# Down-weight sums spread over a forgetting attention, two stores behind the first biases, one transposition moved

## The chip, the cores and the metric

The kernel runs on one core of a Trainium2 chip. A core has TensorE (PE) for matrix products and transpositions, VectorE (DVE), ScalarE (ACT), GpSimd (POOL) and SyncE (SP). Each engine works through its own list of instructions in order; semaphores hold an instruction until what it reads has been written, and until the buffer that it writes is free. SyncE issues transfers here, and GpSimd issues some too; both kinds run on the same 16 DMA engines. The metric is the device time of one execution in microseconds (us), as the median over runs.

## The reference

The kernel computes a trunk of two decoder layers over 512 tokens of 1024 features, in float32:

```python
for l in range(DEPTH):                      # DEPTH = 2
    g = norm_gains[l]
    if l < N_A:                             # layer 0: dilated sliding-window attention
        mix = dilated_mixer(rms_norm(h, g[0]), w_qkv_a[l], w_o_a[l], cos, sin)
    else:                                   # layer 1: forgetting attention on shared keys, values
        if l == N_A:
            kvf = rms_norm(h, kv_norm) @ w_kvf
            k_sh, v_sh = ...
            c_sh = cumsum(log_sigmoid(kvf[..., 2048:] + b_f))
        mix = fox_mixer(rms_norm(h, g[0]), w_q_b[j], w_o_b[j], k_sh, v_sh, c_sh)
    h = h + rms_norm(mix, g[1])
    f = conv_ffn(rms_norm(h, g[2]), w_up[l], conv_w[l], conv_b[l], w_down[l])
    h = h + rms_norm(f, g[3])
```

`fox_mixer` has 16 heads of 64. Scores are q k / 8 plus the difference of two cumulative gates c, causal, followed by a softmax, by p v and by the product with `w_o`. `conv_ffn` is an up-projection to 2 x 2816 columns, a causal convolution of width 3 over the tokens, gelu(gate) times value, and a down-projection.

## The kernel before

**Products.** Each float32 operand is kept as a rounded part and a rest, and a product is three matmuls (lines 276 to 278 in `mm3`). ScalarE casts a loaded weight to its rounded part (L56), and VectorE subtracts to get the rest (L64). In the attention of layer 1 the rest is made another way: ScalarE writes the negative (L58), and an accumulating DMA from GpSimd's queue adds the raw weight to it (`low_added`, L81). Class `Weights` loads the pieces in their order of use, on SyncE's queue (L48).

**Down-weight sums.** The down-projection of each FFN is computed for some blocks with sums of weight blocks, so that fewer matmuls are needed. `down_sums` is a generator that prepares them, one pair of 128-row blocks `(l, j)` after another. A pair takes three loads on SyncE's queue (L601 to L603, 1 MB in all), four subtractions of 128x512 on VectorE (L606 to L609) and two stores of 512 KB to a DRAM buffer `dT` (L614). Its last arguments are the queue of the stores and two lags, in calls of `next`: from the loads to the subtractions (`lag`), and from these to the stores (`behind`). The sums are read from `dT` in the down stage of the FFN, much later.

**The order of the work is written out by hand.** The program is one sequence, and every instruction goes to its engine's list in the order of the program. In the first attention `wide_proj` computes a projection in four steps of two weight pieces each and calls a list of other functions after each step: transpositions of q and k, scores with their softmax, and `p_transpose` (four transpositions of probabilities into a PSUM bank, L1097, and a copy by ScalarE, L1099). Scores are read by VectorE from PSUM (L1060) and exponentiated by ScalarE (L1061).

**The forgetting attention** (L1646 to L1782). Head pairs j = 0 to 7 have four blocks of 128 queries each. A loop over m runs two blocks at a time: m = 2j for blocks 0 and 1, m = 2j + 1 for blocks 2 and 3, with two steps more at the end. In one step come

- at even m a load of the gates c of the next head pair, broadcast to all partitions (`load_ck`, L1440),
- scores (`f_scores`, L1663), and p v of the step m - 2 (`f_pv`, L1710),
- VectorE adding the bias and taking the row maximum (`f_exp`, L1671), ScalarE's exponential (L1673),
- GpSimd building the bias of the next step, -c_k + c_q under the causal mask (`f_bias`, L1644 and L1645),
- query projections of later head pairs (`q_part`, matmuls into `q_ps`, results in `qst`),
- the normalization (L1681, L1683), transposition (L1695) and copy (L1697) of probabilities,
- from step 13 on the first products with `w_o` (`po.both`, tile `acc`).

Ahead of the loop, `f_bias(0, 0)` and `f_bias(0, 1)` build the first two biases.

**Behind the attention** come the conv rows (four loads of 22 KB, L578 and L579, transposed by TensorE at L586), two gains (L221), the rest of the product with `w_o` (`po.finish`) and, with its results, a `Boundary`: row statistics on ScalarE (L316, L318), the residual stream h (L330), its norm (L283, L285), xn (L295) and the transpositions of xn (L344), from which the FFN of layer 1 starts. ScalarE and VectorE split the first weight pieces of `w_up` ahead of these statistics.

**Sums of layer 1 before the change.** Pairs 0 and 1 are prepared in the key projections just ahead of the attention, with GpSimd's queue for the stores and `behind = 0`, so a pair's stores come in the same call as its subtractions. Pairs 2 to 5 are prepared by one generator, also with GpSimd's queue and `behind = 0`: the loop calls it at m = 13 to 16, and it is called once more behind the conv rows' loads.

Of the kernel before, what the change touches and what calls it, by code (L numbers as in the profile page):

```python
# [100 lines left out]
def trunk_kernel(ctx, tc, x, norm_gains, w_qkv_a, w_o_a, w_q_b, w_o_b, kv_norm, w_kvf, b_f,  # L101
                 w_up, conv_w, conv_b, w_down, rope, out):
    nc = tc.nc
    act, dve, pool, pe, sp = nc.scalar, nc.vector, nc.gpsimd, nc.tensor, nc.sync
# [11 lines left out]
    def t4(shape, dt=F32, name="t4"):  # L116
        return p4.tile(shape, dt, tag="t4", name=name)
# [473 lines left out]
    def down_sums(pairs, place, queue, lag, behind):  # L591


        live, n = [], len(pairs)
        for i in range(n + lag + behind):
            if i < n:
                l, j = pairs[i]
                a, b = place()
                live.append((a, b))
                r = w_down[l][j * 256:j * 256 + 256, :].rearrange("(c p) d -> c p d", p=128)  # L600
                sp.dma_start(a, r[0])  # L601
                sp.dma_start(b[:, 0:512], r[1, :, 512:1024])
                sp.dma_start(b[:, 512:1024], r[1, :, 0:512])  # L603
            if 0 <= i - lag < n:
                a, b = live[i - lag]
                dve.tensor_tensor(a[:, 0:512], a[:, 512:1024], a[:, 0:512], ALU.subtract)  # L606
                dve.tensor_tensor(a[:, 512:1024], b[:, 0:512], a[:, 512:1024], ALU.subtract)
                dve.tensor_tensor(b[:, 0:512], b[:, 0:512], a[:, 0:512], ALU.subtract)
                dve.tensor_tensor(b[:, 512:1024], b[:, 512:1024], b[:, 0:512], ALU.subtract)  # L609
            i -= lag + behind  # L610
            if i >= 0:
                l, j = pairs[i]
                for q, t in enumerate(live[i]):
                    queue.dma_start(dT[l][j, :, q * 1024:q * 1024 + 1024], t)  # L614
            yield
# [578 lines left out]
    L = later  # L1194
# [51 lines left out]
    sums = down_sums([(1, 6), (1, 7)], in_two, sp, 1, 3)  # L1246
# [22 lines left out]
    def v_post(g, b, o):  # L1269
        if b == 0:  # L1270
# [19 lines left out]
        [L(qk_transpose, 2, 0), L(qk_transpose, 2, 1), L(p_transpose, 1, 2)],  # L1290
        [L(qk_transpose, 2, 2), L(qk_transpose, 2, 3), L(p_transpose, 1, 3), lambda: W.split(W.n_get + 3),
         L(scores, 2, 0), L(scores, 2, 1)],
        [L(scores, 2, 2), L(scores, 2, 3), L(p_transpose, 2, 0)],
        [factors, L(p_transpose, 2, 1), L(p_transpose, 2, 2), L(p_transpose, 2, 3)]], 1)
    for g in range(2):
        for pr in range(2):
# [140 lines left out]
    def load_ck(j, queue=sp):  # L1437
        t = t4([128, 2, T], name="ck")
        s = cd[2 * j:2 * j + 2, :]
        queue.dma_start(t, bass.AP(tensor=s.tensor, offset=s.offset, ap=[[0, 128], [T, 2], [1, T]]))  # L1440
        cks[j] = t
# [4 lines left out]
    def q_part(j, i):  # L1446

        if j >= 8:
            return
        if i == 0:  # L1450
            qps[j] = (bank([128, T], name="q_ps"), [t.rearrange("p (k c) -> p k c", k=8) for t in W.get()])
        o, (wh, wl) = qps[j]
        for kc in (2 * i, 2 * i + 1):
            bh, bl = xs(xTq, kc, ALL)
            mm3(o, wh[:, kc, :], wl[:, kc, :], bh, bl, kc == 0, kc == KD - 1)
# [4 lines left out]
    def q_high(j):  # L1460
        if j >= 8:
            return
        if j % 2 == 0:
            qT[j // 2] = t8([128, 2, 2, T], F32R, name="qst")
        act.copy(query_parts(j)[0], qps[j][0])

    def q_low(j):
        if j >= 8:
            return
        hi, lo = query_parts(j)  # L1470
        dve.tensor_tensor(lo, qps.pop(j)[0], hi.bitcast(F32), ALU.subtract)
# [128 lines left out]
                mm3(vc[bp], ah, al, w4[s][0][:, k, :], w4[s][1][:, k, :], False, False, True)  # L1600
        keep_values(0, bp, vc[bp])
    del w4
    down1 = down_sums([(1, j) for j in range(2)], in_two, pool, 1, 0)
    for c in range(4, 8):
        if c == 7:
            for i in range(4):
# [32 lines left out]
    def f_bias(j, i):  # L1639
        n = (i + 1) * 128  # L1640
        bias = t4([128, 2, T], name="bias")
        for hh in range(2):
            hd = 2 * j + hh
            pool.tensor_scalar(bias[:, hh, :n], cks[j][:, hh, :n], -1.0, cq[:, i, hd:hd + 1], ALU.mult, ALU.add)  # L1644
        pool.affine_select(bias[:, :, n - 128:n], bias[:, :, n - 128:n], pattern=[[0, 2], [-1, 128]],  # L1645
                           compare_op=ALU.is_ge, fill=NEG, base=0, channel_multiplier=1)  # L1646
        bia[j, i] = bias

    def f_scores(j, i0):

        if i0 == 0:
            o = [bank([128, 2, 256], name="s_ps") for _ in range(2)]
            s = [[o[hh][:, i] for hh in range(2)] for i in range(2)]
        else:
            s = [[bank([128, T], name="s_ps") for _ in range(2)] for _ in range(2)]
        q, k = query_parts(j), key_parts(j)
        for i in range(2):
            nn = max((i0 + i + 1) * 128, 256)
            qs = slice((i0 + i) * 128, (i0 + i + 1) * 128)
            for n, (a, b) in enumerate(((0, 0), (1, 0), (0, 1))):  # L1660
                for hh in range(2):
                    rows = slice(64 * hh, 64 * hh + 64)
                    pe.matmul(s[i][hh][:, :nn], q[a][rows, qs], k[b][rows, :nn], start=n == 0, stop=n == 2)  # L1663
        return s

    def f_exp(j, i, s):
        n = (i + 1) * 128
        p = bia.pop((j, i))
        nm, ls = small(2, "nm"), small(2, "ls")
        for hh in range(2):  # L1670
            dve.tensor_tensor_reduce(p[:, hh, :n], s[hh][:, :n], p[:, hh, :n], -0.125, BIG, ALU.add, ALU.min,  # L1671
                                     nm[:, hh:hh + 1])
            act.activation(p[:, hh, :n], p[:, hh, :n], AF.Exp, bias=nm[:, hh:hh + 1], scale=-1.0,  # L1673
                           accum_out=ls[:, hh:hh + 1])
        prob[j, i] = (p, ls)

    def f_norm(j, i):
        n = (i + 1) * 128
        p, ls = prob[j, i]
        rl = small(2, "rl")  # L1680
        dve.reciprocal(rl, ls)  # L1681
        for hh in range(2):
            dve.tensor_scalar(p[:, hh, :n], p[:, hh, :n], rl[:, hh:hh + 1], None, ALU.mult)  # L1683
# [19 lines left out]
    def f_pv(j, i):  # L1703
        if i == 0:
            ops[j] = bank([128, T], name="o_ps")
        o = ops[j]
        for k in range(i + 1):
            for hh in range(2):
                hd = 2 * j + hh
                pe.matmul(o[64 * hh:64 * hh + 64, i * 128:(i + 1) * 128],  # L1710
                          Vt[hd // 8][:, k, (hd % 8) * 64:(hd % 8) * 64 + 64], pT[j, i, hh][:, k, :],
                          start=k == 0, stop=k == i)
        del pT[j, i, 0], pT[j, i, 1]

    def f_out_high(j):
        o = ops[j]
        if j % 2 == 0:
            OTb[j // 2] = t8([128, 2, 2, T], F32R, name=f"OTb{j // 2}")
        t = OTb[j // 2]
        act.copy(t[:, 0, j % 2, :], o)  # L1720
# [13 lines left out]
            W.split(W.n_get + 1)  # L1734
    f_bias(0, 0)
    f_bias(0, 1)
    M = len(pairs)
    down1 = down_sums([(1, j) for j in range(2, 6)], in_one, pool, 1, 0)
    for m in range(M + 2):
        live = m < M  # L1740
        if live:
            j, i0 = pairs[m]
            if i0 == 0 and j + 1 < 8:
                load_ck(j + 1)
            s = f_scores(j, i0)
        if m >= 2:
            ju, iu = pairs[m - 2]
            f_pv(ju, iu)
            f_pv(ju, iu + 1)
        if live:  # L1750
            for a in range(2):
                f_exp(j, i0 + a, s[a])
            if i0 == 2 and j < 6:
                W.low_added()
        if m >= 2 and iu == 2:
            f_out_high(ju)
        for a in range(2):
            i = i0 + a
            if live:
                if m + 1 < M:  # L1760
                    f_bias(pairs[m + 1][0], pairs[m + 1][1] + a)
                q_part(j + 1 + (i > 0), (i + 3) % 4)
                if i == 0:
                    q_high(j + 1)
                f_norm(j, i)
            if 1 <= m <= M:
                f_transpose(pairs[m - 1][0], pairs[m - 1][1] + a)
            if 0 <= 2 * m + a - FILL < len(fill):
                po.both(*fill[2 * m + a - FILL])
            if live and (j, i) >= (6, 2):  # L1770
                W.low()
            if live and (j, i) >= (6, 1) and W.n_split < wo + 4:
                W.high()
        if live and i0 == 0:
            q_low(j + 1)
            if j < 6:
                W.high(minus=True)
        if live and i0 == 2 and j:
            f_out_low(j - 1)
        if M - 3 <= m <= M:  # L1780
            next(down1)

    f_out_low(7)
    W.ahead, W.ahead_dma = 4, 2
    cp = conv_columns(load_conv(1))
    next(down1)
    bd = Boundary(load_gain(norm_gains[1, 1], "gain11"), load_gain(norm_gains[1, 2], "gain12"), "xc")
    po.finish(bd, 4)

# [44 lines left out]
```

## Time and profile before

| | us |
|---|---|
| median of three runs | 1116.37 (1115.2 to 1116.7) |
| the profiled execution | 1118.54 |
| its span | 1116.7 |
| TensorE busy | 1103.4 (99%) |
| VectorE busy | 894.4 (80%) |
| ScalarE busy | 617.0 (55%) |
| GpSimd busy | 191.1 (17%) |
| forgetting attention | about 622 to 728 |
| longest wait of TensorE | 2.14, at 755.5 |

Times in the profile count from the start of the span. An answer on waits names the waiting engine, tile and line, then what released it, then us in total, times, longest. A row of the timeline has start, duration, engine, line, operation, tiles and shapes, count, and in brackets the idle time of the engine before it with its releaser. A row of the chain has start, duration and what ran. Where equal instructions follow each other, a row stands for all of them. "SPq" and "POOLq" are the queues of DMAs that these engines issue.

### The profile page before, as it was taken

The numbers are of one execution on the slowest core, as the hardware profiler recorded it, in microseconds if no ns is written. First come the engines' busy times: TensorE is split into PE (matmuls) and PEld (weight loads), VectorE is DVE, ScalarE is ACT, GpSimd is POOL, SyncE is SP. The second block draws the span as 40 slices with busy tenths as digits, with TensorE's granted clock in tenths as the row PEclk, the third lists the DMA queues.
The fourth block names the chain that finished last, engine by engine and source line by source line (L and its number), as shares of the span: only waits on it lengthen the run. The fifth ranks groups of instructions, "written<-read, shape, count | busy, mean of one in ns | idle before, by whom it ended". The sixth has DMA issues, their size and how long they took to land.

```text
span 1116.7 us, 17530 instructions
## 1 busy us (share of the span) xinstructions
PE 1103.4 (99%) x6395; PEld 942.6 (84%) x6395; DVE 894.4 (80%) x1462; ACT 617.0 (55%) x1038; POOL 191.1 (17%) x287
## 2 busy tenths in 40 slices
PE   9999999999999999999999999999999999999997
PEld 6988889889889888888888788878889889887886
DVE  6677778888888699997877766968888888689995
ACT  5444565545445457576564677745545445456573
POOL 1832100300000121000010555401300000121000
PEclk9999999999999999999999999999999999999999
DMA  9469854333443599884772654894333443599962
GB/s 323 152 212 402 339 165 134 95 105 113 135 123 121 151 358 364 319 315 99 208 153 76 207 125 123 284 285 132 95 108 110 135 124 120 156 345 367 324 245 75
DMA packets 180464, 218.40 MB, mean 196 GB/s; under 512 B 11225, under 2 KB 131017, under 8 KB 180378
## 3 DMA queue, kind: packets, MB, share of 16 engines
q1 hardware_dynamic: 168698, 180.81, 49.5%
q0 software_dynamic: 11680, 36.48, 11.4%
q8 instruction: 50, 0.82, 0.3%
q14 instruction: 36, 0.29, 0.1%
HBM read 170.28 MB, written 39.63 MB: 188 GB/s over the span
## 4 chain that ended last, share of the span: by engine, by line
PE 90%; DMA 4%; ACT 2%; DVE 2%; issue 1%; SPq 1%; POOL 0%; DVEq 0%; ACTq 0%; POOLq 0%
PE up L276 12%; PE up L277 12%; PE up L278 12%; PE acc L276 8%; PE acc L278 8%; PE acc L277 8%; DMA dsums<-in_w_down_dram 2%; PE qk_ps L277 2%; PE qk_ps L276 2%; PE qk_ps L278 2%; PE v_ps L276 2%; PE v_ps L277 2%; PE v_ps L278 2%; PE o_ps L1710 2%; PE pT_ps L1695 2%; PE s_ps L1663 1%
## 5 line engine op out<-in xcount | busy, mean ns | idle before, releaser
L640 ACT ACTIVATE bb<-up,conv 128x512 f32<-128x512 f32 x80 | 60.6, 775 | 148.4 <-DVE up L972 76.2
L64 DVE TENSOR_TENSOR w<-wraw,w 128x1024 fp32r<-128x1024 f32 x94 | 121.3, 1319 | 23.8 <-ACT w L56 23.4
L278 PE MATMUL acc<-w 128*128 128x512 f32 (+1 forms) x311 | 120.5, 387 | 1.1 <-DVE w L768 1.1
L276 PE MATMUL acc<-w 128*128 128x512 f32 (+1 forms) x311 | 120.5, 388 | 0.0
L56 ACT CAST w<-wraw 128x1024 fp32r<-128x1024 f32 x108 | 110.4, 1049 | 17.1 <-DMA wraw<-in_w_up_dram 8.8
L276 PE MATMUL up<-xbh,w 128*128 128x512 f32 (+1 forms) x292 | 104.9, 359 | 0.0
L277 PE MATMUL up<-xbl,w 128*128 128x512 f32 (+1 forms) x292 | 104.8, 359 | 0.0
L276 PE MATMUL up<-xch,w 128*128 128x512 f32 (+1 forms) x292 | 104.8, 359 | 0.0
L277 PE MATMUL up<-xcl,w 128*128 128x512 f32 (+1 forms) x292 | 104.8, 359 | 0.0
L278 PE MATMUL up<-xbh,w 128*128 128x512 f32 (+1 forms) x292 | 104.7, 358 | 0.0
L278 PE MATMUL up<-xch,w 128*128 128x512 f32 (+1 forms) x292 | 104.7, 358 | 0.0
L277 PE MATMUL acc<-w 128*128 128x512 f32 (+1 forms) x267 | 103.3, 387 | 0.0
L656 POOL DMA_DIRECT2D hD<-hc x42 | 24.2, 576 | 318.0 <-DVE hc L658 316.6
L278 PEld LDWEIGHTS acc<-w 128*128 128x128 f32 x311 | 58.4, 188 | 13.4 <-DVE w L768 1.5
L276 PEld LDWEIGHTS acc<-w 128*128 128x128 f32 x311 | 58.4, 188 | 11.9
L641 DVE SCALAR_TENSOR_TENSOR bb<-up,conv,bb 128x511 f32<-128x511 f32 x80 | 59.4, 743 | 7.8 <-ACT bb L640 7.8
L276 PE MATMUL up<-xsh,w 128*128 128x256 f32 x224 | 63.4, 283 | 0.0
L277 PE MATMUL up<-xsl,w 128*128 128x256 f32 x224 | 63.4, 283 | 0.0
L278 PE MATMUL up<-xsh,w 128*128 128x256 f32 x224 | 63.4, 283 | 0.0
L276 PEld LDWEIGHTS up<-xch,w 128*128 128x128 f32 x292 | 55.1, 189 | 8.3
L276 PEld LDWEIGHTS up<-xbh,w 128*128 128x128 f32 x292 | 55.1, 189 | 8.3
L643 DVE SCALAR_TENSOR_TENSOR bb<-up,conv,bb 128x510 f32<-128x510 f32 x80 | 59.9, 749 | 2.8
(325 smaller groups left out, 3031.5 us busy)
## 6 DMA issues: line engine op xcount, KB each, us to landing
wraw<-in_w_up_dram SPq DMA_DIRECT2D x88, 512.0 KB, 4.3
dT<-dsums SPq DMA_DIRECT2D x24, 512.0 KB, 6.0
dsums<-in_w_down_dram SPq DMA_DIRECT2D x22, 512.0 KB, 6.2
dsums<-in_w_down_dram SPq DMA_DIRECT2D x44, 256.0 KB, 7.0
hD<-hc POOLq DMA_DIRECT2D x44, 256.0 KB, 4.8
dact<-hD SPq DMA_DIRECT2D x44, 256.0 KB, 5.9
wraw<-dT SPq DMA_DIRECT2D x22, 512.0 KB, 6.9
wraw<-in_w_down_dram SPq DMA_DIRECT2D x22, 512.0 KB, 5.9
```

The lines of the kernel that those rows point to most:

```text
L56: self.nc.scalar.copy(pair[:, 0], raw)
L64: self.nc.vector.tensor_tensor(pair[:, 1], raw, pair[:, 0].bitcast(F32), ALU.subtract)
L276: pe.matmul(o, ah, bh, start=first, stop=False, skip_group_check=shared)
L277: pe.matmul(o, ah, bl, start=False, stop=False, skip_group_check=shared)
L278: pe.matmul(o, al, bh, start=False, stop=last, skip_group_check=shared)
L640: act.activation(bb[:, s, :], ps, AF.Identity, bias=cp[:, 3, ch:ch + 1], scale=cp[:, 2, ch:ch + 1])
L641: dve.scalar_tensor_tensor(bb[:, s, 1:], ps[:, :T - 1], cp[:, 1, ch:ch + 1], bb[:, s, 1:], ALU.mult, ALU.add)
L643: dve.scalar_tensor_tensor(bb[:, s, 2:], ps[:, :T - 2], cp[:, 0, ch:ch + 1], bb[:, s, 2:], ALU.mult, ALU.add)
L656: pool.dma_start(hD[c - 1], hc.pop(c - 1))
L1663: pe.matmul(s[i][hh][:, :nn], q[a][rows, qs], k[b][rows, :nn], start=n == 0, stop=n == 2)
L1695: pe.transpose(o[:, k0 + k, :], p[:, hh, k * 128:(k + 1) * 128], ident)
L1710: pe.matmul(o[64 * hh:64 * hh + 64, i * 128:(i + 1) * 128], Vt[hd // 8][:, k, (hd % 8) * 64:(hd % 8) * 64 + 64], pT[j, i, hh][:, k, :], st ...
```

## The change

1. In the third `wide_proj`, `p_transpose(2, 0)` goes from behind `scores(2, 2)` and `scores(2, 3)` to ahead of them.
2. The generator of pairs 0 and 1 gets `behind = 1`. The stores of a pair then come one call after its subtractions. The stores of pair 1 come in a further call, placed behind `f_bias(0, 0)` and `f_bias(0, 1)`.
3. Pairs 2 to 5 get a generator each, with SyncE's queue for the stores and `behind = 1`. Pair 2 is loaded at the end of step m = 2, subtracted at the end of m = 4 and stored at the end of m = 5; pair 3 has m = 5, 7 and 8, pair 4 m = 8, 10 and 11, pair 5 m = 14, 16 and 17. The call behind the conv rows goes.

The numbers of loads, subtractions and stores stay the same. Eight stores go from GpSimd's queue to SyncE's.

```diff
-        [L(scores, 2, 2), L(scores, 2, 3), L(p_transpose, 2, 0)],
+        [L(p_transpose, 2, 0), L(scores, 2, 2), L(scores, 2, 3)],
...
-    down1 = down_sums([(1, j) for j in range(2)], in_two, pool, 1, 0)
+    down1 = down_sums([(1, j) for j in range(2)], in_two, pool, 1, 1)
...
     f_bias(0, 0)
     f_bias(0, 1)
+    next(down1)
     M = len(pairs)
-    down1 = down_sums([(1, j) for j in range(2, 6)], in_one, pool, 1, 0)
+    sums = {}
+    for j, m in ((2, 2), (3, 5), (4, 8), (5, 14)):
+        g = down_sums([(1, j)], in_one, sp, 1, 1)
+        for i in (m, m + 2, m + 3):
+            sums.setdefault(i, []).append(g)
...
-        if M - 3 <= m <= M:
-            next(down1)
+        for g in sums.get(m, ()):
+            next(g)
...
     cp = conv_columns(load_conv(1))
-    next(down1)
```

## The prediction

> **What bounds the kernel now.** I read the page's busy shares first, then the waits of TensorE, then the stretches around each wait, the DMA traffic there, and the chain that ended last.
>
> ```profile
> PE 1103.4 (99%) x6395; PEld 942.6 (84%) x6395; DVE 894.4 (80%) x1462; ACT 617.0 (55%) x1038; POOL 191.1 (17%) x287
> ```
> ```profile
> PE xt_ps L344 <- DVE xn L295: 2.1, 1, 2.1
> ...
> PE acc L278 <- DVE w L768: 1.1, 1, 1.1
> ...
> PE pT_ps L1097 <- DVE st L1060: 0.8, 1, 0.8
> PE o_ps L1710 <- ACT pT L1697: 0.7, 1, 0.7
> ```
>
> TensorE is busy for 99% of the span, and the change neither adds nor removes a matmul. So a gain can only come out of the few waits above (total us, times, longest), and a loss can only be a new wait of TensorE. The change touches the surroundings of three of the four: 2.1, 0.8 and 0.7. The 1.1 belongs to the second FFN's down stage, which no edit touches.
>
> The largest wait, at 755.5 us, comes at the end of a stretch in which the DMA engines are full:
>
> ```profile
> 634.00:700.00 66.00, 66.00 (x548) 53.52 (x547) 45.60 (x160) 51.96 (x137) 38.11 (x70) 1.00 0.50 129
> 700.00:728.00 28.00, 28.00 (x246) 22.77 (x246) 25.43 (x65) 18.83 (x48) 11.19 (x20) 1.00 0.83 290
> ```
> ```profile
> dT<-dsums POOLq DMA_DIRECT2D x8, 512.0 KB, 8.4
> wraw<-in_w_up_dram SPq DMA_DIRECT2D x6, 512.0 KB, 10.1
> ...
> dsums<-in_w_down_dram SPq DMA_DIRECT2D x4, 512.0 KB, 4.6
> dsums<-in_w_down_dram SPq DMA_DIRECT2D x8, 256.0 KB, 7.4
> ```
> ```profile
> 747.39 1.06 ACT w L56
> ...
> 755.51 0.66 PE xt_ps L344 x4
> ...
> 756.97 0.43 PE acc L276
> ...
> 759.53 0.43 PE acc L276
> ...
> 760.25 0.23 PE acc L278
> ```
>
> The first fence gives two stretches (the last columns are the granted clock, the share of the DMA engines and GB/s), the second the transfers from 700 to 757 us (KB each, median us to landing), the third pieces of the chain. Loads and stores of the down-weight sums are 4 x 0.5 + 8 x 0.25 + 8 x 0.5 = 8 MB, beside 3 MB of w_up. A w_up load takes 10.1 us, ScalarE's cast of it holds up the boundary's statistics (L316, L318), and these hold up xn: TensorE stands 2.14 us and then runs seven matmuls (756.97 to 759.53) at 0.43 instead of 0.23, so the stall also cost about 7 x 0.20 = 1.4 us of half clock.
>
> [...]
>
> **The change part by part.**
>
> *One transposition moved (wide_proj 3).* p_transpose(2,0) goes ahead of scores(2,2) and (2,3).
>
> ```profile
> 125.88 1.04 ACT L56 CAST w<-wraw 128x1024 fp32r<-128x1024 f32 x1
> 128.74 0.63 PE L1097 MATMUL pT_ps<-ident,p 128*128 128x128 f32 x4 [0.85 <-DVE st L1060]
> 131.58 0.57 ACT L1099 COPY PT<-pT_ps 128x512 f32<-128x512 f32 x1
> ```
>
> It waits 0.85 us for a PSUM bank that VectorE reads at L1060. Earlier in the order it gets a bank that is already free, and its input was exponentiated before the cast at 125.88. Its own copy (0.57) falls on ScalarE right after that cast, about 126.9 to 127.9 with its latency, and only the last scores, due near 128.0, want that bank. Worth between 0 (the wait moves to those scores) and -0.85; I take **-0.85**, as the copy ends before its due time.
>
> *First biases ahead of two stores.* The two 512 KB stores of pair (1,1) are issued by GpSimd after f_bias(0,0) and f_bias(0,1), which they precede now.
>
> ```profile
> DMA to landing us min/median/max: 3.7/4.5/5.2
> ```
> ```profile
> 620.71 0.53 POOL L614 DMA_DIRECT2D dT<-dsums  x1 [4.76 <-DVE dsums L607]
> ...
> 622.74 0.86 POOL L1644 TENSOR_SCALAR bias<-ck,cq 128x128 f32<-128x128 f32 x2
> ...
> 624.07 0.93 POOL L1644 TENSOR_SCALAR bias<-ck,cq 128x256 f32<-128x256 f32 x2
> ```
> ```profile
> 618.87 0.21 DVE L1630 COPY cq<-cq_ps 128x64 f32<-128x64 f32 x1
> ...
> 625.51 0.42 DVE L1671 CUSTOM_DVE_ANT_0 bias<-s_ps,bias 128x256 f32<-128x256 f32 x1 [0.89 <-POOL bias L1645]
> ```
> ```profile
> 632.47 0.83 ACT L1697 COPY pT<-pT_ps 128x256 f32<-128x256 f32 x2
> ```
>
> The biases need cq (619.1) and the first ck row, which is issued in the same program step and whose loads landed in 3.7 to 5.2 us (first fence, ck L1440); the trace has it issued at 614.9, so it is there by 620.1. A bias takes 1.3 us (622.74 to 624.07), so both are done by 622.8 against 625.5. The stores leave a few tenths later at most, and nothing reads them before the down stage. VectorE's second pair moves from 625.51 to about 623.9, and ScalarE's copy at 632.47 by about as much. TensorE wanted it at 632.13. Bounds 0 to -0.74; I take **-0.74**, since 1.6 us of lead is twice the wait.
>
> *The sums of pairs 2 to 5 spread (m = 2, 5, 8, 14 instead of 13 to 16).* Three of four pairs, 6 MB, leave the full stretch for one at half DMA share (129 GB/s). What then lies ahead of the four w_up casts from 724.5 on is a store, two gains, three w_o and four w_up loads, 5 MB, at 290 GB/s 17 us: the last lands near 741.7, and its cast ends near 742.8 instead of 748.45.
>
> ```profile
> 744.82 0.39 PE L278 MATMUL acc<-w,OTb 128*128 128x512 f32 x1
> ```
> ```profile
> 748.92 0.58 ACT L316 ACTIVATE junk<-acc 128x512 bf16<-128x512 f32 x1
> ```
>
> The statistics then wait for TensorE alone, which finishes the first block at about 745.1. From the second L316 to the transposition it took 755.51 - 748.92 = 6.6 us, so xn is ready near 751.7, and TensorE gets there at 755.51 - 2.14 = 753.4: 1.7 us to spare, and more than 2 for the casts. I take the whole wait and its clock, -2.14 - 1.4 = **-3.54**. Bounds 0 (the rival below) and -3.85 (two transpositions, at 0.66 for four instead of 0.44, had the half clock too, with a row to spare).
>
> What it costs on VectorE: four subtractions of a pair take 2.9 us, now at m = 4, 7, 10 and 16.
>
> ```profile
> 652.30 0.56 DVE L1671 CUSTOM_DVE_ANT_0 bias<-s_ps,bias 128x384 f32<-128x384 f32 x1 [1.96 <-PE s_ps L1663]
> ...
> 672.13 0.29 DVE L1671 CUSTOM_DVE_ANT_0 bias<-s_ps,bias 128x128 f32<-128x128 f32 x1 [0.59 <-issue]
> ...
> 713.79 0.68 DVE L606 TENSOR_TENSOR dsums<-dsums 128x512 f32<-128x512 f32 x1
> ...
> 723.75 0.69 DVE L609 TENSOR_TENSOR dsums<-dsums 128x512 f32<-128x512 f32 x1
> ```
> ```profile
> 674.91 0.87 ACT L1697 COPY pT<-pT_ps 128x384 f32<-128x384 f32 x2
> ```
> ```profile
> 677.23 1.49 PE L1663 MATMUL s_ps<-kst,qst 64*128 64x384 f32 x12
> ```
> ```profile
> 654.36 0.87 POOL L81 DMA_DIRECT2D w<-wraw  x1 [5.63 <-ACT w L58]
> ```
>
> At even m they fall into an idle 1.96 us (652.30), and ScalarE, which follows, has casts to do until just before 654.36 (L58, which releases the L81 row): nothing. At m = 7 only 0.59 us is free before 672.13, so the exponentials of j = 4 come 2.9 - 0.6 = 2.3 us later, and with them the copies behind them on ScalarE. The first of these ended at 674.91 + 0.44 = 675.35 (half of 0.87) and would end at 677.65; the scores that take its bank start at 677.23. I take the difference, **+0.45** (0 to 1: ScalarE may make some up, or the second copy be late too). At m = 16 TensorE waits for nothing, and VectorE does this work there now: 0.
>
> What it costs on SyncE's queue: eight stores move to it from GpSimd's. Those of pairs 2 to 4 wait for VectorE and hold back ck and w_q loads behind them by 1 to 4 us, but a ck row is wanted a whole pair later, and five pairs take the 66 us from 634 to 700: nothing. Those of pair 5 stand ahead of the conv rows, two gains, three w_o and six w_up loads.
>
> ```profile
> 719.58 0.38 SPq L579 DMA_DIRECT2D cv_rows<-in_conv_b_dram  x1
> ```
> ```profile
> 728.22 0.44 PE L586 MATMUL cv_ps<-ident,cv_rows 44*128 44x44 f32 x4
> ```
> ```profile
> cd<-c POOLq DMA_DIRECT2D x1, 32.0 KB, 2.2
> ```
>
> The second store waits for L609, which ends at 724.44; the four conv rows then go out by 726.0, about 6 us later than today, and TensorE transposes them at 728.22 ahead of everything behind it. The nearest row for a small transfer, 32 KB, landed in 2.2 us; the longest ck load in 5.2. The stall lies between 0 and 726.0 + 5.2 - 728.22 = 3.0. I take **+0.3**, nearest to the small transfer.
>
> [...]
>
> *Sum*: -0.85 - 0.74 - 3.54 + 0.45 + 0.3 = **-4.4 us**. The profiled execution took 1118.54 (its span 1116.7) and would take 1114.1. It is 2.2 above the median of the runs, 1116.37, which goes to **1112.0**.
>
> **The rivals.**
>
> *The w_up loads are late all the same* (their issue waits for the conv rows, gains and w_o behind the store). The 3.54 stays: 1116.37 - 0.85 - 0.74 + 0.75 = 1115.5. It decides if the last cast ends past 746.3 (753.4 less the 7.1 us that it took from that cast's end, 748.45, to the transposition). Against it: 742.8, at a rate that had the sums' traffic in it. Chance 0.12.
>
> *The conv rows come late.* With 3.0 us at L586 the half clock would follow, as after 2.14: 3.0 + 1.4 - 0.3 above the forecast, 1116.1. [...] Chance 0.14, half of it under 1114.1.
>
> *The half clock stays, whatever the wait does*: 1.4 more, 1113.4. For it: the waits of 0.7 and 0.8 us brought no such matmuls, so a short wait alone need not. Against: it begins right behind the longest wait. Chance 0.06. [...]
>
> *Slower: the accumulating weight DMAs collide with the sums.*
>
> ```profile
> 662.41 0.40 PE L278 MATMUL q_ps<-xqh,w 128*128 128x512 f32 x1
> ```
> ```profile
> DMA to landing us min/median/max: 4.5/8.1/11.9
> ```
>
> In the attention these (L81) land in 4.5 us, with 662.41 - 654.36 - 4.5 = 3.5 to spare. The stores and the next loads, 2 MB, now go out near 653 to 657. Where the DMA is full elsewhere they take up to 11.9: a stall of 3.9, with the clock 5.3. Once, that eats the gain (1117.3); at two of the three bunches, 1122.6. From 6.6 us of such stall the change is slower. Against: the share of 0.50 leaves room for 2 MB in 13 us. Chance 0.12.
>
> **How the numbers follow.** The forecast has 0.56. 0.2% of the time, 2.2 us, is about what a measurement of this kernel can tell from no change. Faster: 0.56 + 0.06 + 0.07 = 0.69. Same: 0.12 + 0.07 = 0.19. Slower: 0.12. The forecast's own range is 1110.8 to 1113.0; the range given reaches from 1110.7 (no cost at all, -5.4 or 1110.9, and a little scatter) to 1116.6, which takes in the late weights and the late conv rows.
>
> **What the profile after would show.** The wait for xn L295 and the row at half clock are gone, the four w_up casts end before 746 in today's time, and the share of DMA from 700 to 745 falls. Wrong would be: a wait of cv_ps L586, a wait of q_ps L278 on an L81 transfer, or the boundary still behind ScalarE's casts.

## The result, and the profile after

| | us (median) | runs |
|---|---|---|
| before | 1115.38 | 22 |
| after | 1113.95 (1113.39 to 1115.4) | 22 |

The ratio is 0.9986, with a 95% interval of 0.998 to 0.9993: 1.4 us faster. That is inside the range of the prediction and on the side that it named, but 1.9 us short of 1112.0: a third of the 4.4 us that it added up. It is also less than the 2.2 us from which the prediction counted a change as faster, so by its own division this is the outcome "same", to which it gave 0.19. With 22 runs the interval is narrow enough to exclude no change. That the time lies in the range says little, since 1110.7 to 1116.6 holds the 1115.38 of before as well. The median of before is lower than the 1116.37 that the prediction started from, which was the median of only three runs. The execution behind the first profile, 1118.54, was as long as the longest of the 22 (1118.55).

The profiled execution of after took 1115.4 (span 1113.5), 3.1 us less than that of before; it too was the longest of its 22. These are some of its waits of TensorE:

```profile
PE q_ps L278 <- DMA w<-wraw: 1.2, 2, 0.9
...
PE s_ps L1663 <- ACT pT L1697: 0.6, 1, 0.6
PE v_ps L277 <- DVE w L1485: 0.2, 1, 0.2
PE acc L278 <- DVE w L768: 0.2, 1, 0.2
```

The three waits that the change aimed at are gone: pT_ps L1097, o_ps L1710 and xt_ps L344. Two kinds are new. TensorE waits twice for a weight from an accumulating DMA (L81), and once for ScalarE's copies. In the timeline and the chain of after, the second of the DMA waits and the copies' wait are these:

```profile
662.72 0.51 PE L278 MATMUL q_ps<-xqh,w 128*128 128x512 f32 x1 [0.28 <-DMA w<-wraw]
678.69 1.57 PE L1663 MATMUL s_ps<-kst,qst 64*128 64x384 f32 x11 [0.57 <-ACT pT L1697]
```
```profile
653.94 0.29 issue
654.22 8.46 DMA w<-wraw
662.68 0.04 issue
662.72 0.51 PE q_ps L278
```

The stretches (TensorE, its weight loads, DVE, ACT, POOL, clock, DMA share, GB/s) show how the traffic moved:

```profile
634.00:700.00 66.00, 64.22 (x536) 51.36 (x533) 50.62 (x159) 49.10 (x127) 37.25 (x67) 1.00 0.74 218
700.00:728.00 28.00, 28.00 (x230) 22.47 (x224) 21.72 (x64) 20.47 (x54) 9.41 (x16) 1.00 0.38 132
728.00:757.00 29.00, 29.00 (x155) 24.17 (x155) 18.83 (x27) 16.90 (x28) 0.00 (x0) 1.00 0.71 202
```

From 700 to 728 the share of the DMA engines falls from 0.83 to 0.38, and from 728 to 757 TensorE is busy throughout. In the attention (634 to 700) the share rises from 0.50 to 0.74, and TensorE loses 1.8 us there, where it lost nothing.

### The profile page after: what moved, and what is told of

The parts are those of the page before. It is cut to its first block, busy times and chain, and to the rows that moved or that the text cites. A ratio compares the mean times of both kernels' runs of the same rounds, so it can differ in the third digit from the quotient of the medians.

```text
span 1113.5 us, 17517 instructions
## 1 busy us (share of the span) xinstructions
PE 1102.7 (99%) x6395; PEld 942.3 (85%) x6395; DVE 894.6 (80%) x1462; ACT 617.0 (55%) x1038; POOL 190.3 (17%) x279
## 4 chain that ended last, share of the span: by engine, by line
PE 86%; DMA 6%; DVE 3%; issue 2%; ACT 2%; POOL 0%; DVEq 0%; SPq 0%; POOLq 0%; ACTq 0%
PE up L276 12%; PE up L277 12%; PE up L278 12%; PE acc L276 8%; PE acc L278 8%; PE acc L277 8%; DMA dact<-hD 3%; PE qk_ps L277 2%; PE qk_ps L276 2%; PE qk_ps L278 2%; PE o_ps L1710 1%; DMA w<-wraw 1%; PE first L276 1%; PE first L278 1%; PE first L277 1%
## 5 line engine op out<-in xcount | busy, mean ns | idle before, releaser
L64 DVE TENSOR_TENSOR w<-wraw,w 128x1024 fp32r<-128x1024 f32 x94 | 121.5, 1315 | 21.6 <-ACT w L56 21.1
L278 PE MATMUL acc<-w 128*128 128x512 f32 (+1 forms) x311 | 120.5, 388 | 0.2 <-DVE w L768 0.2
L278 PE MATMUL up<-xch,w 128*128 128x512 f32 (+1 forms) x292 | 104.7, 359 | 0.0
L278 PE MATMUL up<-xbh,w 128*128 128x512 f32 (+1 forms) x292 | 104.7, 359 | 0.0
L278 PEld LDWEIGHTS acc<-w 128*128 128x128 f32 x311 | 58.4, 188 | 12.5 <-DVE w L768 0.6
L278 PE MATMUL up<-xsh,w 128*128 128x256 f32 x224 | 63.4, 283 | 0.0
```

The source lines that it names most:

```text
L64: self.nc.vector.tensor_tensor(pair[:, 1], raw, pair[:, 0].bitcast(F32), ALU.subtract)
L278: pe.matmul(o, al, bh, start=False, stop=last, skip_group_check=shared)
```

## The experiments

Each time is the median of its runs; the ratio is to runs of the kernel before on the same chip.

### A second trace of the kernel before

No edit.

> The kernel before, once more, for a second trace of it. Theory 1 (the profiled execution stands for all): the waits of TensorE are those of the first trace, 2.1 us for xn L295 and seven matmuls at half clock behind it, and its time is within 0.2 us of the kernel before. Theory 2 (that execution was a long one, 3.2 us above the median of 22 runs): the wait for xn is shorter by 1 us or more, or no matmul behind it runs at 0.43, and the span is about 1113.5 to 1115.

Measured: 1115.69 us, ratio 1.0002 (0.9994 to 1.0011). The wait for xn was even longer, but the matmuls behind it, in the chain, were at full speed:

```profile
PE xt_ps L344 <- DVE xn L295: 2.6, 1, 2.6
```
```profile
757.02 0.66 PE xt_ps L344 x4
757.68 0.23 PE acc L276
757.91 0.23 PE acc L277
```

So both theories hold in part. The wait is there in both traces; the half clock, 1.4 us of the prediction's sum, came in the first only. In the two kernels below that leave the sums in place the same wait is 0.7 and 1.9. Four executions thus had 2.1, 2.6, 0.7 and 1.9, and the half clock once. Three of the four took longer than the median of their kernel, by 3.2, 2.2 and 0.8 us; the one with 0.7 took 0.7 us less. So a usual execution may wait less than these traces show.

### Only the transposition moved

```diff
-        [L(scores, 2, 2), L(scores, 2, 3), L(p_transpose, 2, 0)],
+        [L(p_transpose, 2, 0), L(scores, 2, 2), L(scores, 2, 3)],
```

> Only p_transpose(2, 0) is moved. Theory 1: the wait of 0.85 us at L1097 is gone and nothing takes its place in the following 20 us: -0.85 us, ratio 0.9992. Rival: the last scores wait for ScalarE's copy instead, and the time stays (ratio 1.0000).

Measured: 1115.28 against 1116.01, ratio 0.9994 (0.9985 to 1.0002). In the trace the wait at L1097 is gone and nothing follows in its place:

```profile
PE acc L278 <- DVE w L768: 0.9, 1, 0.9
PE o_ps L1710 <- ACT pT L1697: 0.8, 1, 0.8
PE xt_ps L344 <- DVE xn L295: 0.7, 1, 0.7
```

The trace shows the rival wrong. The time by itself, 0.7 us, is not clear of zero.

### Only the first biases ahead of the stores

```diff
-    down1 = down_sums([(1, j) for j in range(2)], in_two, pool, 1, 0)
+    down1 = down_sums([(1, j) for j in range(2)], in_two, pool, 1, 1)
...
     f_bias(0, 1)
+    next(down1)
```

> Only the first biases go ahead of the stores of pair 1. Theory 1: the wait of 0.74 us at L1710 is gone: -0.7 us, ratio 0.9993. Rival: with the attention earlier, TensorE reaches the weight that the accumulating DMA (L81) adds up, and waits there: 0.4 to 0.9 us at q_ps L278 near 636, the time stays (ratio 1.0000). If the wait at L278 is absent here, it needs the early loads of pair 2 too.

Measured: 1115.16 against 1116.01, ratio 0.9992 (0.9982 to 1.0001). The wait at L1710 is gone, and no matmul waits at q_ps L278, but its weight load does, for 0.45 us. The first accumulating DMA takes 6.3 us to land here, without any early load of pair 2, against 5.4 in the first trace of the kernel before and 4.9 in the second. A load of w_q now leaves 1.8 us behind its issue. The first fence is this kernel, the second the kernel before, where the accumulating DMA was issued at 629.81:

```profile
629.40 0.90 POOL L81 DMA_DIRECT2D w<-wraw  x1
...
631.22 0.38 SPq L48 DMA_DIRECT2D wraw<-in_w_q_b_dram  x1
```
```profile
635.26 0.38 SPq L48 DMA_DIRECT2D wraw<-in_w_q_b_dram  x1
```

So this edit alone uses up nearly all the slack near 636. With the loads of pair 2 there too, the changed kernel and three versions of it below take 6.4 to 7.3 us and wait 0.1 to 0.9. The wait does not need those loads: the version below with all pairs at even steps loads pair 2 only at m = 4, and its matmul still waits 0.3 us here. The time again is not clear of zero by itself.

### Only the sums of pairs 2 to 5 spread

Parts 1 and 2 of the change undone.

> Only the sums of pairs 2 to 5 are spread. Theory 1 (the first trace of before stands for all executions): the wait for xn and its half clock go, -3.5 us, and new waits near 663 and 678 of 0.3 and 0.6 us come: -2.7 us, ratio 0.9976. Theory 2 (most executions of the kernel before have less of that wait): -0.5 to -1.5 us, ratio 0.9987 to 0.9996, while the profiles differ by about 2.7 us or more.

Measured: 1116.08 against 1116.01, ratio 1.0001 (0.9993 to 1.001). The part from which the prediction had most of its gain is worth nothing, less than either theory gave it. The wait for xn is gone, and in its place stands another:

```profile
664.69 0.50 PE L278 MATMUL q_ps<-xqh,w 128*128 128x512 f32 x1 [1.84 <-DMA w<-wraw]
```
```profile
664.00:670.00 6.00, 5.31 (x30) 4.23 (x32) 0.80 (x3) 2.69 (x4) 1.77 (x3) 0.72 0.44 130
```

TensorE stands 1.84 us for an L81 transfer, and the half clock followed here (mean granted clock 0.72 from 664 to 670). A wait near the end was exchanged for one of the same kind in the attention. This execution took 1117.95, 1.9 us above the median; it is one of two of the eleven runs with a mean granted clock of 0.997, and the nine others, at 0.998 or 0.999, have a median of 1115.6. So the half clock is not what brings the ratio to 1.0001, and how long a usual execution waits here, no trace shows. The gain of the whole change, 1.4 us, is about that of its other two parts, 0.7 + 0.85 = 1.6 us.

### The changed kernel once more

No edit to the changed kernel.

> The changed kernel once more, on the chip and beside the runs of the next three. If the sums' own worth is nil and the gain is that of the other two edits (0.9994 and 0.9992 apart), the ratio is 0.9986 again. Its trace should show waits of q_ps L278 on the accumulating DMA near 636 and 663, of a different length than the first trace's 0.9 and 0.3 (0 to 1.9), and no wait for xn of L295.

Measured: 1114.73 against 1115.55, ratio 0.9992 (0.9983 to 1.0001). The new waits are there again, with other lengths: 0.1 near 635, 0.5 near 662, and 0.6 at s_ps L1663. None for xn.

### Pair 3 at even steps

```diff
-    for j, m in ((2, 2), (3, 5), (4, 8), (5, 14)):
+    for j, m, n in ((2, 2, 3), (3, 6, 4), (4, 8, 3), (5, 14, 3)):
...
-        for i in (m, m + 2, m + 3):
+        for i in (m, m + 2, m + n):
```

> As the changed kernel, but pair 3 is loaded at the end of m = 6, subtracted at m = 8 and stored at m = 10. The stores of pair 2 near 653 stay, and the loads of pair 3 no longer stand there. Theory A (the loads and the stores together hold up the accumulating DMA of 654): the wait near 663 goes, and with VectorE free at m = 7 the wait of s_ps L1663 near 678 goes too: 0.6 to 1.5 us below the changed kernel, ratio 0.9973 to 0.9981. Theory B (the 1 MB of stores alone holds it up, or the DMA's length comes from something else): the transfer still lands after 7 us or more, and only the 0.6 us at m = 7 goes: 0.9981.

Measured: 1112.56 on the same chip as the run above (1114.73), ratio 0.9974 (0.9965 to 0.9983). Theory A was right, though 2.2 us is more than the 0.6 to 1.5 that it gave. These are the waits of TensorE that the trace lists, and the first two stand at the start of the kernel:

```profile
PE warm L237 <- DVE zero L232: 1.4, 1, 1.4
PE qk_ps L277 <- DVE w L64: 0.7, 2, 0.5
PE q_ps L278 <- DMA w<-wraw: 0.3, 1, 0.3
```

One pair, loaded and subtracted one step later and stored two steps later, is worth 2.2 us. About 0.7 of it may come from elsewhere: the trace of the changed kernel's second run waits 0.7 us at acc L278 in the second FFN, this one does not. In the changed kernel the stores of pair 2 and the loads of pair 3 stand around the accumulating DMA:

```profile
651.53 1.78 SPq L614 DMA_DIRECT2D dT<-dsums  x2
653.36 0.45 SPq L601 DMA_DIRECT2D dsums<-in_w_down_dram  x1
653.87 0.77 SPq L602 DMA_DIRECT2D dsums<-in_w_down_dram  x1
...
654.22 0.88 POOL L81 DMA_DIRECT2D w<-wraw  x1 [5.64 <-ACT w L58]
...
654.68 0.46 SPq L603 DMA_DIRECT2D dsums<-in_w_down_dram  x1
```

The accumulating DMA issued near 654 took the following times to land. The first fence is the kernel before, the second the changed kernel, the third this one:

```profile
w<-wraw POOLq DMA_DIRECT2D x1, 512.0 KB, 4.5
```
```profile
w<-wraw POOLq DMA_DIRECT2D x1, 512.0 KB, 8.5
```
```profile
w<-wraw POOLq DMA_DIRECT2D x1, 512.0 KB, 6.3
```

Without sums beside it 4.5 us; with the stores of pair 2 alone 6.3; with stores of 1 MB and loads of 1 MB 8.5 (8.7 in the second trace), and 10.0 in the kernel with only the sums spread. TensorE wanted it about 8.1 us after its issue. No run has the loads alone beside it, and why 10.0 is more than 8.5 stays open.

### All pairs at even steps

```diff
-    for j, m in ((2, 2), (3, 5), (4, 8), (5, 14)):
+    for j, m in ((2, 4), (3, 6), (4, 8), (5, 10)):
...
-        for i in (m, m + 2, m + 3):
+        for i in (m, m + 2, m + 4):
```

> As the changed kernel, but all four pairs go by even steps: loads at the end of m = 4, 6, 8, 10, subtractions two steps later, stores four steps later. Loads and stores then leave SyncE's queue right behind the weight loads near 645, 658, 671, about 9 us ahead of the next accumulating DMA, and no sums are subtracted at odd m. Theory A (collisions with the accumulating DMA and VectorE's odd step ate what the boundary gave): no wait of q_ps L278 above 0.3 us, none of s_ps L1663, none for xn L295: 1.5 to 3.0 us below the changed kernel, ratio 0.996 to 0.9973. Rival (the sums are worth nothing wherever they are put, because moving 6 MB out of the end only moves the contention): at most 0.3 us below the changed kernel, 0.9984 or more, with a wait elsewhere.

Measured: 1117.25, ratio 1.0014 (1.0004 to 1.0023): slower than before. Theory A had the waits that go right and the time wrong. The rival's numbers hold, 0.9984 or more and a wait elsewhere, but its reason does not: the last version below keeps three of the four pairs at these steps and is fast. The collisions near 654 and 678 are gone (0.3 us at L278 near 635 is left), but a wait stands elsewhere:

```profile
PE acc L277 <- DVE w L64: 2.7, 1, 2.7
```
```profile
700.29 0.67 DVE dsums L606
...
700.98 0.86 DVE dsums L607
...
701.87 0.86 DVE dsums L608
...
705.81 1.28 DVE bias L1683 x2
707.09 1.35 DVE w L64
```

In the chain of waits pair 5's subtractions, now at m = 12, come ahead of VectorE's split of the first w_o piece, for which TensorE waits 2.7 us, again with the half clock (0.43 us for a matmul at acc from 709.28 on, 0.23 at 716.30). Ten of the eleven runs have a mean granted clock of 0.996 or 0.997, so here it seems to have come nearly every time.

### The stores on GpSimd's queue

```diff
-        g = down_sums([(1, j)], in_one, sp, 1, 1)
+        g = down_sums([(1, j)], in_one, pool, 1, 1)
```

> As the changed kernel, but the stores of pairs 2 to 5 go by GpSimd's queue. If the move to SyncE's queue matters by itself: SyncE's loads no longer wait behind the subtractions, the conv rows leave about 6 us earlier, but GpSimd's queue holds the biases back behind the stores, as ahead of the attention. Theory A: the queue makes no difference beyond 0.5 us, since both run on the same DMA engines and the waits near 636 and 663 stay (ratio 0.9982 to 0.9990). Theory B: biases late behind a store cost a new wait of 0.7 us or more of TensorE at o_ps or s_ps (ratio 0.9992 or more).

Measured: 1116.8, ratio 1.0009 (1.0 to 1.0017), 2.1 us above the changed kernel on the same chip. The sign is theory B's, the place another one. In the chain:

```profile
656.94 0.45 POOL bias L1645
...
657.45 0.53 POOL dT L614
...
658.04 7.53 DMA dT<-dsums
...
665.63 0.41 ACT w L56
```

On GpSimd's queue the stores of pair 2 leave at 657.45, behind the biases, against 651.53 to 653.3 on SyncE's queue in the first trace of the changed kernel. Their buffer comes free at 665.6, a cast on ScalarE waits 1.4 us for it, and the chain goes on from there over the exponentials to waits of TensorE of 0.5 and 1.1 us near 677, where the changed kernel has 0.6; the half clock follows (28 matmuls at o_ps L1710 take 2.19 us at 681.43, and 1.68 at 694.88). So the queue does matter, by what is ahead of the store in its engine's order. The 2.1 us are not one size: five of the eleven runs, the traced one among them, have a mean granted clock of 0.997 and a median of 1117.6; the other six have 0.998 or more and 1115.6, which is 0.8 us above the changed kernel. In this trace neither these stores nor the loads of pair 3 stand near the accumulating DMA of 653, and it landed in 4.6 us.

### Pair 3 again, and three variants of it beside each other

The version with pair 3 at even steps, unedited:

> The version with pair 3 at m = 6, 8, 10 once more, beside the next three: ratio 0.9974 within 0.0010, no wait of TensorE from 640 to 760 above 0.3 us.

Measured: 1112.56 against 1115.99, ratio 0.9965 (0.9952 to 0.9978). Only 0.4 us at L278 near 636 is left as a wait.

Pair 3 loaded at m = 5 as in the change, but subtracted at m = 8 and stored at m = 9:

```diff
-    for j, m in ((2, 2), (3, 5), (4, 8), (5, 14)):
+    for j, steps in ((2, (2, 4, 5)), (3, (5, 8, 9)), (4, (8, 10, 11)), (5, (14, 16, 17))):
...
-        for i in (m, m + 2, m + 3):
+        for i in steps:
```

> As the changed kernel, but pair 3, still loaded at m = 5, is subtracted at m = 8 and stored at m = 9. It parts the two costs that the version above took away together. If the loads beside the stores near 653 are what holds up the accumulating DMA: it lands 8 us or more after 653 again, the wait near 662 stays (0.3 to 1.8 us), and the wait of s_ps L1663 near 678 is gone: 0.5 us below the changed kernel, ratio 0.998 to 0.9987. If VectorE's odd step were the whole cost: no wait near 662 either, ratio 0.9974.

Measured: 1113.78, ratio 0.9977 (0.9968 to 0.9986). The wait at s_ps L1663 is gone. The accumulating DMA takes 8.6 us to land, and 0.45 us of wait near 662 stays. On the same chip this is 1.2 us above the version that loads at m = 6 and stores at m = 10, each one step later, which is what the place of these transfers is worth by itself. The odd step's 0.6 is shown by the trace alone, since the changed kernel did not run beside these.

Parts 1 and 2 undone, with pair 3 at even steps:

```diff
-    for j, m in ((2, 2), (3, 5), (4, 8), (5, 14)):
+    for j, steps in ((2, (2, 4, 5)), (3, (6, 8, 10)), (4, (8, 10, 11)), (5, (14, 16, 17))):
...
-        for i in (m, m + 2, m + 3):
+        for i in steps:
```

> Only the sums of pairs 2 to 5 are spread, with pair 3 at m = 6, 8, 10; the transposition and the biases stay as in the kernel before. If the spreading is worth the boundary's wait once nothing collides: the waits of 0.85 at L1097 and 0.74 at L1710 stay, none for xn and none near 663: ratio 0.9988 (0.9980 to 0.9994), against 1.0001 with pair 3 at odd steps. If the three edits don't add up, it stays at 1.0000.

Measured: 1113.55, ratio 0.9976 (0.9967 to 0.9986). Spreading the sums is worth 2.4 us once nothing collides, more than expected. The trace has one wait that the prediction had named as a sign of being wrong:

```profile
PE cv_ps L586 <- DMA cv_rows<-in_conv_b_dram: 0.5, 1, 0.5
```

Pairs 2, 3 and 4 at even steps, pair 5 as in the change:

```diff
-    for j, m in ((2, 2), (3, 5), (4, 8), (5, 14)):
+    for j, steps in ((2, (4, 6, 8)), (3, (6, 8, 10)), (4, (8, 10, 11)), (5, (14, 16, 17))):
...
-        for i in (m, m + 2, m + 3):
+        for i in steps:
```

> Pairs 2, 3 and 4 by even steps (loads at m = 4, 6, 8; subtractions at 6, 8, 10; stores at 8, 10 and 11), pair 5 as in the changed kernel (14, 16, 17). If the loss of the all-even version came from pair 5's subtractions at m = 12 alone, ahead of VectorE's first split of w_o: the 2.7 us at acc L277 near 708 are gone, and with the wait near 636 also smaller the time is at or below that of the version with pair 3 at m = 6: ratio 0.9968 to 0.9976. If it came from the even steps as such: 1.000 or more.

Measured: 1113.21, ratio 0.9973 (0.9964 to 0.9982). The 2.7 us near 708 are gone, so the loss of the all-even version was pair 5's (the only other difference is that pair 4 is stored at m = 11 and not 12). The wait near 636 is gone too, and the accumulating DMA lands in 4.5 us as in the kernel before. The time can't be told from that of the version with pair 3 alone (0.9965, intervals overlap). These two are the fastest kernels of the study, about 3 us below before.

## Why the prediction was right or wrong

**The transposition (-0.85): right.** The wait went, and nothing took its place. The time, -0.7, agrees, within an interval that includes zero.

**The first biases (-0.74): right, with one duration off.** The wait at L1710 went; -0.85 us, again with an interval that includes zero. Both biases were to be done by 622.8. They were done at 624.1: the second one's pair of instructions took 2.4 us, not the 0.93 us of before. In the rows below, the window ends ahead of the pair's second instruction.

```profile
620.49 0.73 POOL L1645 TENSOR_SCALAR_AFFINE_SELECT bias<-bias 128x256 f32<-128x256 f32 x1
621.22 1.95 POOL L1644 TENSOR_SCALAR bias<-ck,cq 128x256 f32<-128x256 f32 x1
```

They now ran beside VectorE's subtractions (L609 and the split L64). The lead was enough all the same. The two stores left about 3 us later (from 624.20 on, against 620.71 and 622.16), not a few tenths, and nothing waited for them. What the step did not ask is what is late next: a load of w_q now runs beside the first accumulating DMA, and TensorE met that DMA 0.1 to 0.9 us too early.

**The boundary (-3.54): the mechanism right, the size too large.** The wait for xn went in every kernel with spread sums. These rows of after show the end of the last of the four w_up casts (746.0), xn, and the transposition that waited before:

```profile
744.97 1.05 ACT L56 CAST w<-wraw 128x1024 fp32r<-128x1024 f32 x1 [0.71 <-DMA wraw<-in_w_up_dram]
```
```profile
752.42 1.41 DVE L295 SCALAR_TENSOR_TENSOR xn<-h,rs,gain 128x512 f32<-128x512 f32 x2
```
```profile
754.77 1.04 PE L344 MATMUL xt_ps<-ident,xn 128*128 128x128 f32 x8
```

In this execution TensorE comes here 1.6 us later than in the first trace (cv_ps at 729.78, then 728.22). So 746.0 is 744.4 in the time of before: later than the 742.8 of the prediction, but well inside its limit of 746.3. The first half of xn is done at about 753.1, 1.6 us ahead of the transposition; the prediction had 1.7. The size came from one execution. In four, the wait was 0.7, 1.9, 2.1 and 2.6, and the half clock came once: 1.8 us of wait and 0.35 of clock on the mean, 2.2 in place of 3.54, and less if a usual execution waits less. The bound of -3.85 does not follow from its rows either. Four of these transpositions take 0.66 at full clock too (757.02 in the second trace); in the first trace the half clock began with the second four:

```profile
756.17 0.80 PE xt_ps L344 x4
```

Without collisions 2.4 us was measured, but not all of that need be the boundary's. The prediction took the 1.1 us at acc L278 in the second FFN as out of reach. That wait is 0.9 to 1.2 in the four traces with the sums in place, 0.2 and 0.7 in the two of the changed kernel, 1.1 with the stores on GpSimd's queue, and not listed in the seven others, which all have the sums spread on SyncE's queue. Why it shrinks stays open.

**The accumulating DMAs (0 in the sum, a rival with 0.12): the step that failed.** "The share of 0.50 leaves room for 2 MB in 13 us" averaged over a whole pair. The 2 MB go out within 3 us of the accumulating DMA, on the same 16 engines (their busy share from 653 to 657 us is 0.97 in the first trace of the changed kernel, against 0.64 in that of before), and its landing went from 4.5 to 8.5 and 10.0 us against 8.1 that it had. The rival had the place right, and 11.9 us as the far end; the stall was 0.3 to 1.8 near 662, not 3.9. That this, with the odd step below, is what ate the boundary's gain is shown by the edits: with only the sums spread the ratio is 1.0001, and with pair 3 moved away from the DMA and from the odd step it is 0.9976.

**VectorE's odd step (+0.45): the place right, the size by luck.** The wait at s_ps L1663 was 0.57 and 0.60. The subtractions took not 2.9 us but 3.8 (671.9 to 675.65), beside GpSimd's biases. With 3.8 the step's own working gives 0.45 + 0.9, about 1.3 us; where the rest went, it had not counted, and no run shows it. In the timeline:

```profile
671.88 0.85 DVE L606 TENSOR_TENSOR dsums<-dsums 128x512 f32<-128x512 f32 x1
672.77 0.96 DVE L607 TENSOR_TENSOR dsums<-dsums 128x512 f32<-128x512 f32 x1
673.77 0.77 DVE L608 TENSOR_TENSOR dsums<-dsums 128x512 f32<-128x512 f32 x1
674.58 1.07 DVE L609 TENSOR_TENSOR dsums<-dsums 128x512 f32<-128x512 f32 x1
```

**The conv rows (+0.3): no such wait, but of the right order.** They went out 6.6 to 7.6 us later than before, and there is no wait in either trace of the change. The version with pair 3 subtracted at m = 8 and stored at m = 9 has 0.3 us for a weight load at L586, the one with only the sums spread and pair 3 moved has 0.5. The prediction put half of the chance of late rows under 1114.1. No run shows how long a wait at L586 stays free of the half clock: the 0.5 us came in an execution with a mean granted clock of 1.0, and elsewhere 1.84 us brought it (0.72 from 664 to 670 with only the sums spread).

**SyncE's queue.** The prediction saw only a cost in it. Putting the stores back on GpSimd's queue cost 2.1 us by the medians, so the move itself is a gain within this schedule. In the first trace of the changed kernel the conv rows leave right behind pair 5's stores (from 725.38 on, the stores from 723.50), and the waits at L586 of 0.3 and 0.5 us, each in another version, are the most that the traces show of a cost of that.

**The sum.** -0.85 - 0.74 - 2.2 from what goes, +0.6 at the odd step, and 0.6 to 1.2 for the two DMA waits in the two traces gives about -2.0 to -2.6; measured -1.4 (-0.8 to -2.2 by the interval) and -0.8 in the second comparison. If the wait at acc L278 is counted as well, more is left over. What is left, about a microsecond, stays open: the waits come from traces, the medians from other executions, and the wait for xn varies from one execution to the next by more than that. The 2.2 may be too large, since three of its four traces are of executions longer than their medians.

## What to carry to other kernels

A mean DMA share said little here on whether a transfer with a due time would be late: 0.50 over 66 us was read as room, and 2 MB put around one transfer took its landing from 4.5 to 8.5 us, past the 8.1 that it had. Look at which other transfers are issued in the few microseconds around it, and compare its landing with its slack. Work that is moved out of a full stretch has to be put between the transfers that have due times, and on steps where its engine is idle; one pair moved by one or two steps was worth more here (2.2 us) than the whole change (0.8 on the same chip). Before a wait is put into a sum, see it in more than one execution.

## What the runs showed of the hardware

Whether the half clock follows a wait differs between executions. It came after or within these waits of TensorE: 2.1 us in the first trace of the kernel before (granted clock 0.57 from 756 to 760), 1.8 with only the sums spread (0.72 from 664 to 670), 2.7 with all pairs at even steps (matmuls of 0.43 us in place of 0.23), and 0.5 and 1.1 close together with the stores on GpSimd's queue (28 matmuls in 2.19 us in place of 1.68). It did not come after 2.6 in the second trace of the kernel before (matmuls of 0.23 us), nor after 1.9 with only the first biases moved (granted clock 1.00 from 728 to 757). So the length of a wait alone did not decide it here.

VectorE's subtractions and GpSimd's biases took longer beside each other. In the first traces of the kernel before and of the changed kernel, from 612 to 730 us, a subtraction of 128x512 took 0.74 to 1.07 us where it ran beside biases (in the changed kernel from 619.4 to 621.8 and from 671.9 to 675.7) and 0.67 to 0.69 where it did not. One bias instruction beside VectorE's L609 and L64 took 1.95 us (at 621.22 in the changed kernel), where two took 0.93 together before (at 624.07). Why, no trace here shows.
